# An encoder step on one core: first product between x tiles, masks after the q units, norms by pairs, the last norm's end in two passes

## The chip, the core and the metric

The kernel runs on one core of a Trainium2 chip. The metric is the device time of one execution in microseconds (us), as the median of several executions. One execution of each kernel was also taken with the hardware profiler; the views quoted are of that execution. PE is the matrix engine, PEld its weight loads, DVE, ACT and POOL the vector, scalar and general engines, SP the engine that issues most DMAs.

## The reference

One layer of a streaming encoder, on 1024 new frames of one stream and 64 frames of another, 1088 rows of 1024 columns in all. In short:

```python
z = x @ w_in                                  # 1024 -> 8200 columns
glu = z_conv[..., :E] * sigmoid(z_conv[..., E:])
dw = depthwise_conv31(concat(conv_buf, glu)) + b_dw
y_a = silu(layer_norm(dw, ln_a_g, ln_a_b)) @ w_a_out
h, C1, n1, m1 = mlstm(z_q, z_k / 16, z_v, ig, lf, C0, n0, m0)   # 4 heads of 256, chunkwise, causal decay
y_b = (sigmoid(z_o) * head_norm(h) * hn_g) @ w_b_out
merged = sigmoid(g_a) * y_a + sigmoid(g_b) * y_b
x1 = layer_norm(ALPHA * x + merged @ w_out, ln1_g, ln1_b)
ff = square(relu(x1 @ w_ff1)) @ w_ff2         # 1024 -> 4096 -> 1024
x2 = layer_norm(ALPHA * x1 + ff, ln2_g, ln2_b)
```

Everything is float32. The outputs are x2, the convolution's last 30 rows and the states C, n and m of both streams.

## The kernel before, in words

**Products.** Nearly all products are feature-major: the weights are the stationary operand, 128 output features at a time (a unit), and the moving operand is the transposed activations in three chunks of rows, 384, 384 and 320 wide (chunks 0, 1, 2). Float32 accuracy comes from splitting both operands into a high and a low part (`split`: ACT writes the high part, DVE the rest) and three matmuls for each of the eight blocks of 128 inputs (`mm3`), so a product of one unit and one chunk is 24 matmuls. `g` tiles are the three PSUM banks of products, `m` tiles five banks for transposes and small sums.

**Stages.** (1) The start: nine row tiles of x are loaded (pool `xp`, four buffers), transposed on PE and split (`start_x`); the gates' weights `wg` are a tile of the same pool. (2) The input projection, head by head: convolution units, k, q, v and o units, and between their products the chunkwise recurrence of the head (`mlstm`), the convolution on DVE and other work. `head_start` prepares a head's tiles, among them the decay mask `dt`: POOL broadcasts a row over the partitions (L386) and cuts it to a triangle, ACT takes nine exponentials. (3) The b branch's product, during which `ln_a` normalises the convolution's output; then the a branch's product. (4) The output projection (`out_proj`), whose units are the inner loop of each chunk, followed by the first norm of that chunk (`ln1`). (5) The feed-forward in blocks of four units; the first units' chunk 2 is held back until its norm is done. (6) The last block writes row-major tiles of x2 (24 matmuls of 512 columns for each of nine row tiles) with the second norm behind each (`ln_stats`, `ln2_back`).

**The feature-major norm** (`ln_feature`, for `ln_a` and `ln1`) sums over features, which lie on partitions and on eight tiles. DVE adds the eight tiles, PE sums over partitions with a matrix of 1/1024 (L690, L691 for the high and low part), DVE subtracts the mean (L699), ACT squares, DVE adds up the squares (reductions, L678), PE sums them to one column per row (L711, L714), DVE and POOL form the power −0.5 (L716, L717), DVE spreads it over a diagonal (L719), PE broadcasts it (L725, L726), and DVE and ACT scale (L729, L815). It is a generator: each `yield` hands control back for one product, and `waits` holds how many products stand ahead of each of the three PE steps.

**What sets the order.** `N` and `J` line up the jobs; a job's products call `slot()`, which moves the background generators (`mlstm`, `conv`, `misc`) on by a step. A scheduler of the framework then places the instructions on each engine's queue, in an order near that of the program; `pin` keeps an instruction at its place. Each engine works its queue strictly in that order, and waits by semaphores. SP issues the loads: x tiles, weights two units ahead (`wload`), and for `out_proj` one column block of the transposed x per product (`sx`, from pool `st`, five buffers).

Of the kernel before, what the change touches and what calls it, by code (L numbers as in the profile page):

```python
# [49 lines left out]
def hybrid_layer(ctx, tc, x_prompt, x_sample, cache_conv, state_C, state_n, state_m, w_in, b_gate,  # L50
# [101 lines left out]
    xp = pool("xp", 4, stack=st0)  # L152

# [19 lines left out]
    xt0 = [load_x(0), load_x(1)]  # L173

    def start_x():
        for i in range(3):
            trans_x(i, xt0[i])
            if i == 1:
                wsplit(0, True)
        for i in range(3, NT):  # L180
            trans_x(i, load_x(i))
# [19 lines left out]
    def gates():  # L201
# [29 lines left out]
        wg = xp.tile([P, KT, P], F32R, tag="x", name="wg")  # L231
# [78 lines left out]
    early, later = [], []  # L310
# [8 lines left out]
    def unit(hi, lo, post, chunks=(0, 1, 2)):  # L319
        for ci in chunks:  # L320
            ps = early.pop() if early and ci == 0 else product(hi, lo, ci)
# [50 lines left out]
    def head_start(h):  # L372
# [12 lines left out]
        dt = hd.tile([P, NT, P], F32, tag="dt", name="dt")  # L385
# [211 lines left out]
    for h in range(NH):  # L597
# [7 lines left out]
        for j in range(2):  # L605
            add_unit(w_in, 2048 + h * HD + j * P, post_kq("q", j, 1.0))
        for j in range(2):
            add_unit(w_in, 4096 + h * HD + j * P, post_v(j))
# [38 lines left out]
    def ln_stats(tiles, n):  # L647
# [6 lines left out]
        V.scalar_tensor_tensor(st[:n, 16:17], st[:n, 12:13], -1.0, st[:n, 15:16], ALU.mult, ALU.mult)  # L654
        return st[:n, 15:16], st[:n, 16:17]
# [14 lines left out]
    def ln_feature(y, n, sc, square, finish, waits):  # L670
# [6 lines left out]
        def total(out, t, m=CN):  # L677
            V.tensor_reduce(out[:, :n], t[:, :, :n].rearrange("p k t -> p t k"), AX.X, ALU.add)  # L678

        s2 = stp.tile([P, CN], F32, tag="st", name="s2")  # L680
        total(s2, y[:, 0:4])
        yield
        s, sh, sl = tiles()
        total(s, y[:, 4:8])
        V.tensor_tensor(s[:, :n], s[:, :n], s2[:, :n], ALU.add)
        split(sh[:, :n], sl[:, :n], s[:, :n])
# [9 lines left out]
        sq = []  # L696
        for kh in range(2):
            yh = y[:, 4 * kh:4 * kh + 4, :n]
            V.tensor_tensor(yh, yh, across(pm), ALU.subtract)  # L699
            sq.append(square())  # L700
            S.activation(sq[kh][:, :, :n], yh, AF.Square)
        total(s, sq[0])
        total(s2, sq[1])
# [105 lines left out]
    last_ln = []  # L809

    def ln1(ci):
# [12 lines left out]
        yield from ln_feature(Y2[ci], n, pools["ln1"], square, finish, ((1, 3, 2), (1, 3, 1), (1, 2, 1))[ci])  # L824
# [5 lines left out]
    def out_proj():  # L830
# [4 lines left out]
        for ci, (o, n) in enumerate(CHUNKS):  # L835
            Y2.append(fp.tile([P, KT, CN], F32, tag="f", name="y2"))
            for j in range(KT):
# [8 lines left out]
                slot()  # L846
                if ci == 2 and j == 4:
                    last_ln.append(ln1(ci))
                    next(last_ln[0])
            if ci < 2:  # L850
                BG["misc"].append(ln1(ci))
        drain("misc")
        BG["misc"].append(last_ln[0])
# [328 lines left out]
```

## Time and profile before

| | |
|---|---|
| median of three runs | 1987.09 us (1985.12 to 1988.74) |
| the profiled execution's own time | 1988.86 us |
| its span | 1986.8 us |
| PE busy | 1938.1 us, 98% |
| DVE busy | 1425.0 us, 72% |
| ACT busy | 642.8 us, 32% |
| POOL busy | 124.9 us, 6% |
| granted clock of PE, mean | 0.991 |
| last matmul ends | 16 us before the span's end |

The span is the time from the first to the last instruction. The granted clock is the share of full speed that PE was given; a matmul at half clock counts as busy for its whole length. The waits of PE are shown by the line that waited, the engine and line that it waited for, the total, the times and the longest.

### The profile page before, as it was taken

The page shows a single profiled execution, that of the slowest core. Times are in us where ns is not written, and L with a number is a line of the kernel's source. Part 1 is how long each engine was busy: PE and PEld are TensorE (multiplying, and loading weights), DVE is VectorE, ACT ScalarE, POOL GpSimd, SP SyncE. Part 2 cuts the span into 40 slices and gives each one's busy share as a digit, 9 for nine tenths or more (in the row PEclk, how much of TensorE's full clock was granted, in tenths as well). Part 3 has the DMA queues.
Part 4 walks back from the last instruction along what each step waited for, and adds up shares of the span by engine and source line. Part 5 has one row for each costly group of instructions (what it writes and reads, how often), then busy time and mean ns, then how long its engine had stood idle before and what let it go on. Part 6 is the DMA issues. An engine that isn't in the chain of part 4 may idle for free.

```text
span 1986.8 us, 30495 instructions
## 1 busy us (share of the span) xinstructions
PE 1938.1 (98%) x12396; PEld 1914.4 (96%) x12396; DVE 1425.0 (72%) x2717; ACT 642.8 (32%) x1206; POOL 124.9 (6%) x232
## 2 busy tenths in 40 slices
PE   8999999999999999999999998999999999999996
PEld 7999999999999999999999998999999999999995
DVE  3856876787678767878874559867685858677547
ACT  4323322332233223323352214523233232414242
POOL 1112210001000100000000000000000000000005
PEclk9999999999999999999999999999999999999998
DMA  4122312121112211226235210111211111111212
GB/s 140 44 79 58 119 48 57 52 74 52 55 34 66 70 55 43 60 93 205 84 102 158 76 42 14 43 54 33 59 38 54 53 44 54 33 54 43 75 43 80
DMA packets 171744, 131.06 MB, mean 66 GB/s; under 512 B 8271, under 2 KB 166463, under 8 KB 171603
## 3 DMA queue, kind: packets, MB, share of 16 engines
q1 hardware_dynamic: 171603, 129.11, 21.7%
q8 instruction: 97, 1.59, 0.3%
q14 instruction: 44, 0.36, 0.1%
HBM read 104.39 MB, written 24.63 MB: 65 GB/s over the span
## 4 chain that ended last, share of the span: by engine, by line
PE 83%; DVE 9%; issue 3%; ACT 1%; POOL 1%; DMA 1%; SPq 0%; POOLq 0%; ACTq 0%; DVEq 0%
PE g L328 26%; PE g L331 26%; PE g L332 26%; DVE s L678 2%; PE m L328 1%; PE m L332 1%; PE m L331 1%; DVE o L1101 1%; DVE acc L567 1%; DVE ln L650 0%; DVE a L699 0%; DVE y L699 0%; PE m L461 0%; DMA x<-in_x_prompt_dram 0%; PE m L1061 0%
## 5 line engine op out<-in xcount | busy, mean ns | idle before, releaser
L328 PE MATMUL g<-xh,wh 128*128 128x384 f32 (+1 forms) x1920 | 637.7, 332 | 0.0
L331 PE MATMUL g<-xl,wh 128*128 128x384 f32 (+1 forms) x1920 | 632.0, 329 | 0.0
L332 PE MATMUL g<-xh,wl 128*128 128x384 f32 (+1 forms) x1920 | 631.5, 329 | 0.0
L328 PEld LDWEIGHTS g<-xh,wh 128*128 128x128 f32 x1920 | 363.7, 189 | 0.4 <-ACT xh L336 0.2
L331 PEld LDWEIGHTS g<-xl,wh 128*128 128x128 f32 x1920 | 363.5, 189 | 0.3
L332 PEld LDWEIGHTS g<-xh,wl 128*128 128x128 f32 x1920 | 363.1, 189 | 0.1
L567 DVE SCALAR_TENSOR_TENSOR acc<-glu,vecs,acc 128x1118 f32<-128x1118 f32 x240 | 331.6, 1382 | 3.5
L336 ACT ACTIVATE wh<-wr 128x1024 fp32r<-128x1024 f32 (+1 forms) x168 | 166.0, 988 | 445.9 <-PE g L331 355.7
L339 DVE TENSOR_TENSOR wl<-wr,wh 128x1024 fp32r<-128x1024 f32 (+1 forms) x168 | 190.7, 1135 | 113.8 <-ACT wh L336 110.9
L328 PE MATMUL g<-x1h,wh 128*128 128x384 f32 (+1 forms) x768 | 253.4, 331 | 0.0
L331 PE MATMUL g<-x1l,wh 128*128 128x384 f32 (+1 forms) x768 | 253.1, 330 | 0.0
L332 PE MATMUL g<-x1h,wl 128*128 128x384 f32 (+1 forms) x768 | 252.8, 329 | 0.0
L331 PE MATMUL g<-hvl,wh 128*128 128x272 f32 x784 | 223.7, 288 | 0.0
L332 PE MATMUL g<-hvh,wl 128*128 128x272 f32 x784 | 221.9, 288 | 0.0
L328 PE MATMUL g<-hvh,wh 128*128 128x272 f32 x784 | 221.4, 290 | 0.0
L977 DVE TENSOR_TENSOR y<-g,y 128x272 f32<-128x272 f32 (+1 forms) x540 | 157.2, 340 | 26.9 <-PE g L332 25.1
L328 PEld LDWEIGHTS g<-hvh,wh 128*128 128x128 f32 x784 | 146.0, 189 | 1.7 <-DVE y L977 1.3
L331 PEld LDWEIGHTS g<-hvl,wh 128*128 128x128 f32 x784 | 147.5, 188 | 0.0
L332 PEld LDWEIGHTS g<-hvh,wl 128*128 128x128 f32 x784 | 146.5, 188 | 0.0
L331 PEld LDWEIGHTS g<-x1l,wh 128*128 128x128 f32 x768 | 144.9, 189 | 0.1
L332 PEld LDWEIGHTS g<-x1h,wl 128*128 128x128 f32 x768 | 144.9, 189 | 0.0
L328 PEld LDWEIGHTS g<-x1h,wh 128*128 128x128 f32 x768 | 144.6, 188 | 0.1
(272 smaller groups left out, 2423.6 us busy)
## 6 DMA issues: line engine op xcount, KB each, us to landing
wr<-in_w_in_dram SPq DMA_DIRECT2D x64, 512.0 KB
wr<-in_w_ff_dram SPq DMA_DIRECT2D x64, 512.0 KB
x<-in_x_prompt_dram SPq DMA_DIRECT2D x8, 512.0 KB
dwT<-acc SPq DMA_DIRECT2D x8, 512.0 KB
wr<-in_w_b_out_dram SPq DMA_DIRECT2D x8, 512.0 KB
wr<-in_w_a_out_dram SPq DMA_DIRECT2D x8, 512.0 KB
wr<-in_w_out_dram SPq DMA_DIRECT2D x8, 512.0 KB
out_dram<-o SPq DMA_DIRECT2D x16, 256.0 KB
```

The lines of the kernel that those rows point to most:

```text
L328: first = TE.matmul(out, lh, rh, start=start, stop=False, skip_group_check=more)
L331: TE.matmul(out, lh, rl, start=False, stop=False, skip_group_check=more)
L332: TE.matmul(out, ll, rh, start=False, stop=stop, skip_group_check=more)
L336: a = S.activation(hi, src, AF.Copy)
L339: V.tensor_tensor(lo, src, hi.bitcast(F32), ALU.subtract)
L567: V.scalar_tensor_tensor(acc, glu[:, j:j + AC], vecs[:, c, j:j + 1], acc, ALU.mult, ALU.add))
L678: V.tensor_reduce(out[:, :n], t[:, :, :n].rearrange("p k t -> p t k"), AX.X, ALU.add)
L977: V.tensor_tensor(y, ps[:, pslc], y, ALU.add)
L1101: V.tensor_tensor(o[:n, hs], o[:n, hs], pools["g2"][:n, hs], ALU.mult)
```

## The change

In seven places:

- **Start.** `wg` gets a pool of its own. Three x tiles are loaded before the first weights instead of two, the fourth before the second weights instead of the third. The product of the first unit and chunk 0 is issued after tile 2 of x instead of after all tiles, and is kept in `early`, which is now keyed by chunk.
- **Masks.** The decay mask leaves `head_start` and becomes `head_decay`, a job behind the head's q units.
- **Norms by pairs.** In `ln_feature` the reductions over four tiles (`total`) become pairwise additions (`fold`: one add of two tiles' width, one of one tile's), and the first sum begins with one add of four tiles to four.
- **First norm.** `out_proj` keeps a running column sum of each chunk, `ys`, with one add per product, and `ln1` starts from it. The counts in `waits` change, and the third chunk's norm starts behind the last product without a slot of its own.
- **Feed-forward.** The third unit's products of chunk 0 and of chunk 1 are both issued before the held chunk 2 products; before, only that of chunk 0.
- **Second norm.** `ln_stats` returns the mean and the power and drops the product of the two. `ln2_back` forms (y − mean) × g on DVE first, then scales on ACT, then adds b on POOL; for the eighth row tile the add is on DVE, and the ninth is done on DVE alone.

The diff:

```diff
@@ -150,6 +150,7 @@
     negM = cv.tile([P, T], F32, name="negM")
     st0 = ExitStack()
     xp = pool("xp", 4, stack=st0)
+    xg = pool("xg", 1, stack=st0)
 
     def load_x(i):
         xt = xp.tile([P, D], F32, tag="x", name="x")
@@ -170,14 +171,16 @@
             S.activation(hi, ps[:, :, :n], AF.Copy)
             V.tensor_tensor(XL[ci][:, kh * 4:kh * 4 + 4, off:off + n], ps[:, :, :n], hi.bitcast(F32), ALU.subtract)
 
-    xt0 = [load_x(0), load_x(1)]
+    xt0 = [load_x(0), load_x(1), load_x(2)]
 
     def start_x():
-        for i in range(3):
+        for i in range(4):
             trans_x(i, xt0[i])
             if i == 1:
                 wsplit(0, True)
-        for i in range(3, NT):
+            if i == 2:
+                early[0] = product(*his[0], 0)
+        for i in range(4, NT):
             trans_x(i, load_x(i))
         vp = xp.tile([NV, D], F32, tag="x", name="vp")
         nc.sync.dma_start(vp[0:CW, :], w_dw[0])
@@ -228,7 +231,7 @@
         G.memset(mask, 1.0)
         G.memset(mask[:, 0:T:P], 0.0)
         G.memset(cols[SS:, 8], 0.0)
-        wg = xp.tile([P, KT, P], F32R, tag="x", name="wg")
+        wg = xg.tile([P, KT, P], F32R, name="wg")
         G.memset(wg.bitcast(F32), 0.0)
         S.activation(wg[:, :, 0:8], wgr, AF.Copy)
         V.tensor_tensor(wg[:, :, 8:16], wgr, wg[:, :, 0:8].bitcast(F32), ALU.subtract)
@@ -307,7 +310,7 @@
             V.tensor_copy(cols[:n, b:b + nb], ps[:n, 0:nb].rearrange("p c (h z) -> p c h z", z=32)[:, :, :, 0:4])
 
 
-    early, later = [], []
+    early, later = {}, []
 
     def product(hi, lo, ci):
         n = CHUNKS[ci][1]
@@ -318,7 +321,7 @@
 
     def unit(hi, lo, post, chunks=(0, 1, 2)):
         for ci in chunks:
-            ps = early.pop() if early and ci == 0 else product(hi, lo, ci)
+            ps = early.pop(ci) if ci in early else product(hi, lo, ci)
             while later:
                 later.pop()()
             post(ci, *CHUNKS[ci], ps)
@@ -382,7 +385,9 @@
             G.memset(t[:, :, HD + 1:].bitcast(F32), 0.0)
             G.memset(t[SS:, 8, :HD].bitcast(F32), 0.0)
         HT["vh"], HT["vl"] = vh, vl
-        dt = hd.tile([P, NT, P], F32, tag="dt", name="dt")
+
+    def head_decay(h):
+        dt = pools["hd"].tile([P, NT, P], F32, tag="dt", name="dt")
         G.partition_broadcast(dt.rearrange("p c t -> p (c t)")[:, :T], negM[32 * h:32 * h + 1, :])
         G.memset(dt[:, 8, SS:], MASKED)
         G.affine_select(dt, dt, [[0, NT], [1, P]], ALU.is_ge, MASKED, base=0, channel_multiplier=-1)
@@ -604,6 +609,7 @@
             add_unit(w_in, 3072 + h * HD + j * P, post_kq("k", j, 1.0 / 16.0))
         for j in range(2):
             add_unit(w_in, 2048 + h * HD + j * P, post_kq("q", j, 1.0))
+        N(lambda h=h: head_decay(h))
         for j in range(2):
             add_unit(w_in, 4096 + h * HD + j * P, post_v(j))
         if h == 0:
@@ -651,8 +657,7 @@
         V.bn_aggr(st[:n, 12:14], st[:n, 0:12])
         G.tensor_scalar(st[:n, 14:15], st[:n, 13:14], EPS, None, ALU.add)
         G.tensor_tensor(st[:n, 15:16], st[:n, 14:15], mhalf[:n], ALU.pow)
-        V.scalar_tensor_tensor(st[:n, 16:17], st[:n, 12:13], -1.0, st[:n, 15:16], ALU.mult, ALU.mult)
-        return st[:n, 15:16], st[:n, 16:17]
+        return st[:n, 12:13], st[:n, 15:16]
 
 
     A32, MB = [], []
@@ -667,23 +672,25 @@
             MB.append(fp.tile([P, KT, CN], F32, tag="f", name="mb"))
         BG["misc"].append(ln_a())
 
-    def ln_feature(y, n, sc, square, finish, waits):
+    def ln_feature(y, n, sc, square, finish, waits, total=None):
         def across(p, k=4):
             return bcast(p[:, None, :n], [P, k, n])
 
         def tiles():
             return (sc.tile([P, CN], d, tag=t, name=t) for t, d in (("s", F32), ("sh", F32R), ("sl", F32R)))
 
-        def total(out, t, m=CN):
-            V.tensor_reduce(out[:, :n], t[:, :, :n].rearrange("p k t -> p t k"), AX.X, ALU.add)
-
-        s2 = stp.tile([P, CN], F32, tag="st", name="s2")
-        total(s2, y[:, 0:4])
-        yield
+        def fold(out, t):
+            V.tensor_tensor(t[:, 0:2, :n], t[:, 0:2, :n], t[:, 2:4, :n], ALU.add)
+            V.tensor_tensor(out[:, :n], t[:, 0, :n], t[:, 1, :n], ALU.add)
+
         s, sh, sl = tiles()
-        total(s, y[:, 4:8])
-        V.tensor_tensor(s[:, :n], s[:, :n], s2[:, :n], ALU.add)
-        split(sh[:, :n], sl[:, :n], s[:, :n])
+        if total is None:
+            t = square()
+            V.tensor_tensor(t[:, :, :n], y[:, 0:4, :n], y[:, 4:8, :n], ALU.add)
+            fold(s, t)
+            total = s
+            yield
+        split(sh[:, :n], sl[:, :n], total[:, :n])
         for _ in range(waits[0]):
             yield
         pm = mtile()
@@ -693,14 +700,12 @@
         s2 = sc.tile([P, CN], F32, tag="s2", name="s2")
         if n < CN:
             G.memset(s[:, n:], 0.0)
-        sq = []
-        for kh in range(2):
+        for kh, part in enumerate((s, s2)):
             yh = y[:, 4 * kh:4 * kh + 4, :n]
             V.tensor_tensor(yh, yh, across(pm), ALU.subtract)
-            sq.append(square())
-            S.activation(sq[kh][:, :, :n], yh, AF.Square)
-        total(s, sq[0])
-        total(s2, sq[1])
+            sq = square()
+            S.activation(sq[:, :, :n], yh, AF.Square)
+            fold(part, sq)
         V.tensor_tensor(s[:, :n], s[:, :n], s2[:, :n], ALU.add)
         split(sh, sl, s)
         for _ in range(waits[1]):
@@ -806,7 +811,7 @@
 
 
     X1H, X1L, Y2 = [], [], []
-    last_ln = []
+    YS = []
 
     def ln1(ci):
         n = CHUNKS[ci][1]
@@ -821,7 +826,7 @@
 
         def square():
             return pools["lnq" if ci == 2 else "ln1"].tile([P, 4, CN], F32, tag="sq", name="sq")
-        yield from ln_feature(Y2[ci], n, pools["ln1"], square, finish, ((1, 3, 2), (1, 3, 1), (1, 2, 1))[ci])
+        yield from ln_feature(Y2[ci], n, pools["ln1"], square, finish, ((2, 3, 2), (2, 3, 2), (1, 2, 1))[ci], YS[ci])
         if ci == 2:
             lnq.close()
             lns.close()
@@ -843,14 +848,15 @@
                     mm3(ps[:, :n], WOH[j // 4][:, k, js], WOL[j // 4][:, k, js], MH[ci][:, k, :n], ML[ci][:, k, :n],
                         k == 0, k == KT - 1)
                 V.scalar_tensor_tensor(Y2[ci][:, j, :n], s[:, :n], ALPHA, ps[:, :n], ALU.mult, ALU.add)
-                slot()
-                if ci == 2 and j == 4:
-                    last_ln.append(ln1(ci))
-                    next(last_ln[0])
-            if ci < 2:
-                BG["misc"].append(ln1(ci))
-        drain("misc")
-        BG["misc"].append(last_ln[0])
+                if j == 1:
+                    YS.append(stp.tile([P, CN], F32, tag="st", name="ys"))
+                if j:
+                    V.tensor_tensor(YS[ci][:, :n], Y2[ci][:, 0, :n] if j == 1 else YS[ci][:, :n], Y2[ci][:, j, :n], ALU.add)
+                if ci < 2 or j < KT - 1:
+                    slot()
+            if ci == 2:
+                drain("misc")
+            BG["misc"].append(ln1(ci))
         step("misc")
 
     N(out_proj)
@@ -1000,7 +1006,8 @@
             pools["whl"] = pools["whl2"]
             third = 2 + next(i for i, p in enumerate(pieces) if p[3] == 1)
             wsplit(third)
-            early.append(product(*his[third], 0))
+            for ci in range(2):
+                early[ci] = product(*his[third], ci)
             drain("misc")
             for h in held:
                 unit(*h, (2,))
@@ -1092,15 +1099,24 @@
             prev = (i, y, *stats)
         ln2_back(*prev)
 
-    def ln2_back(i, y, rstd, nmr):
+    def ln2_back(i, y, mean, rstd):
         n = tile_len(i)
         o = pools["ln2"].tile([P, D], F32, tag="o", name="o")
         for hf in range(2):
             hs = slice(hf * 512, hf * 512 + 512)
-            S.activation(o[:n, hs], y[:, hs], AF.Identity, bias=nmr, scale=rstd)
-            V.tensor_tensor(o[:n, hs], o[:n, hs], pools["g2"][:n, hs], ALU.mult)
-            (V if i == NT - 1 and hf == 1 else G).tensor_tensor(o[:n, hs], o[:n, hs], pools["b2"][:n, hs], ALU.add)
-            nc.sync.dma_start(y_prompt[0, i * P:(i + 1) * P, hs] if i < 8 else y_sample[0, :, hs], o[:n, hs])
+            if i < NT - 1:
+                V.scalar_tensor_tensor(o[:n, hs], y[:, hs], mean, pools["g2"][:n, hs], ALU.subtract, ALU.mult)
+                S.activation(o[:n, hs], o[:n, hs], AF.Identity, scale=rstd)
+                (V if i == NT - 2 else G).tensor_tensor(o[:n, hs], o[:n, hs], pools["b2"][:n, hs], ALU.add)
+            else:
+                V.scalar_tensor_tensor(o[:n, hs], y[:, hs], mean, pools["g2"][:n, hs], ALU.subtract, ALU.mult)
+                if hf == 1:
+                    for h2 in range(2):
+                        hs = slice(h2 * 512, h2 * 512 + 512)
+                        V.scalar_tensor_tensor(o[:n, hs], o[:n, hs], rstd, pools["b2"][:n, hs], ALU.mult, ALU.add)
+                        nc.sync.dma_start(y_sample[0, :, hs], o[:n, hs])
+                continue
+            nc.sync.dma_start(y_prompt[0, i * P:(i + 1) * P, hs], o[:n, hs])
 
     N(open_last)
     for u in range((NBLK - 1) * NB, NBLK * NB):
@@ -1137,7 +1153,7 @@
 
     idx = 0
     wload(0)
-    xt0.append(load_x(2))
+    xt0.append(load_x(3))
     wload(1)
     for ap, fn, kind, _ in jobs:
         if ap is None:
```

The order of POOL around the second head's start, first before, then of the change. `dt` is the head's mask, `st` the row statistics of the previous head's last tile, `xs` a sum that is written back to memory, `nout` and `vh` state and value tiles.

```order
L377 MEMSET k 128x2x64
L386 ISA
L386 ISA dt<-negM 128x1088
L508 COPY nout<-C 128x2
L364 ISA
L364 TENSOR_TENSOR xs<-xh,xl 128x320
L520 TENSOR_SCALAR st<-st 64x1
L364 TENSOR_TENSOR xs<-xh,xl 128x320
L521 TENSOR_TENSOR st<-st,mhalf 64x1
L381 MEMSET vh 128x9
```

```order
L380 MEMSET k 128x2x64
L391 ISA
L391 ISA dt<-negM 128x1088
L513 COPY nout<-C 128x2
L367 ISA
L367 TENSOR_TENSOR xs<-xh,xl 128x320
L525 TENSOR_SCALAR st<-st 64x1
L367 TENSOR_TENSOR xs<-xh,xl 128x320
L526 TENSOR_TENSOR st<-st,mhalf 64x1
L384 MEMSET vh 128x9
```

The same rows stand at the same places; the line of the mask's broadcast is L391 now, that of the statistics L525 and L526.

The order of DVE in the norm of branch a, chunk 1, from the subtraction of the mean on, before and then of the change. `a` is the chunk (the last tile number is the next chunk), `sq` the squares, `s`, `sh`, `sl` the sum and its parts, `mb` the merged product beside it.

```order
L699 TENSOR_TENSOR a_9287<-a_9287,m 128x1536 x2
L678 TENSOR_REDUCE s<-sq 128x384
L678 TENSOR_REDUCE s_9764<-sq 128x384
L763 TENSOR_TENSOR mb<-g,sb 128x384
L704 TENSOR_TENSOR s<-s,s_9764 128x384
L763 TENSOR_TENSOR mb<-g,sb 128x320
L678 TENSOR_REDUCE s_9953<-a_9289 128x320
L339 TENSOR_TENSOR sl<-s,sh 128x384
L339 TENSOR_TENSOR wl<-wr,wh 128x1024
L763 TENSOR_TENSOR mb<-g,sb 128x384
```

```order
L705 TENSOR_TENSOR a_9291<-a_9291,m 128x1536 x2
L683 TENSOR_TENSOR sq<-sq 128x768
L768 TENSOR_TENSOR mb<-g,sb 128x384
L684 TENSOR_TENSOR s<-sq 128x384
L683 TENSOR_TENSOR sq<-sq 128x768
L689 TENSOR_TENSOR sq<-a_9293 128x4x320
L684 TENSOR_TENSOR s_9770<-sq 128x384
L768 TENSOR_TENSOR mb<-g,sb 128x320
L709 TENSOR_TENSOR s<-s,s_9770 128x384
L342 TENSOR_TENSOR wl<-wr,wh 128x1024
L342 TENSOR_TENSOR sl<-s,sh 128x384
L683 TENSOR_TENSOR sq<-sq 128x2x320
```

Two reductions of the squares and one over the next chunk became pairwise adds; the next chunk's first add (L689) moved ahead of the sum of the squares, and the weight split `wl` ahead of `sl`.

The order of ACT where the output projection ends and the feed-forward begins. `y_11265` and `y_11283` are chunk 1 of the first norm, the higher number chunk 2, `x1h` the high part of the normed chunk, `wh` that of a weight, `r` the relu of a product.

```order
L336 ACTIVATE x1h<-y_11265 128x768
L815 ACTIVATE y_11265<-y_11265,vecs 128x384 x2
L336 ACTIVATE x1h<-y_11265 128x768
L815 ACTIVATE y_11265<-y_11265,vecs 128x384 x2
L336 ACTIVATE x1h<-y_11265 128x768
L815 ACTIVATE y_11265<-y_11265,vecs 128x384
L336 ACTIVATE sh<-s 128x320
L336 ACTIVATE x1h<-y_11265 128x768
L336 ACTIVATE wh<-wr 128x1024
L906 ACTIVATE r<-g 128x384
L336 ACTIVATE wh<-wr 128x1024
L701 ACTIVATE sq<-y_11558 128x4x320 x2
```

```order
L820 ACTIVATE y_11283<-y_11283,vecs 128x384 x2
L339 ACTIVATE sh<-ys 128x320
L339 ACTIVATE x1h<-y_11283 128x768
L820 ACTIVATE y_11283<-y_11283,vecs 128x384 x3
L339 ACTIVATE x1h<-y_11283 128x768
L820 ACTIVATE y_11283<-y_11283,vecs 128x384 x2
L339 ACTIVATE x1h<-y_11283 128x768
L820 ACTIVATE y_11283<-y_11283,vecs 128x384
L339 ACTIVATE wh<-wr 128x1024
L339 ACTIVATE x1h<-y_11283 128x768
L339 ACTIVATE wh<-wr 128x1024
L912 ACTIVATE r<-g 128x384
```

The scaling of chunk 1 is split in the same way in both. The high part of chunk 2's sum (`sh<-s 128x320`, now `sh<-ys 128x320`) moved from behind the chunk's last scaling to behind its second. On PE the broadcast that this scaling waits for moved too: it stood 16 matmuls into chunk 2's last product and the rest of that product followed it, and now it stands behind the whole product.

## The prediction

> **What bounds the kernel now.** I read the page's busy times first, then what PE waited for, then the chain at each wait, then the last 40 us.
>
> ```profile
> span 1986.8 us, 30495 instructions
> PE 1938.1 (98%) x12396; PEld 1914.4 (96%) x12396; DVE 1425.0 (72%) x2717; ACT 642.8 (32%) x1206; POOL 124.9 (6%) x232
> ```
>
> PE sets the end. The change leaves its 12396 matmuls as they are, so it can gain only what PE does not spend on matmuls at full clock: 1986.8 − 1938.1 = 48.7 us idle, and the stretches at half clock, which count as busy. The waits of PE by line (us in total, how often, the longest):
>
> ```profile
> PE m L445 <- DVE isb L523: 7.0, 3, 2.5
> PE m L168 <- DMA x<-in_x_prompt_dram: 6.6, 3, 4.8
> PE m L714 <- DVE sl L339: 4.8, 3, 2.3
> PE m L711 <- ACT sh L336: 4.7, 2, 2.9
> PE m L725 <- ACT sh L336: 2.0, 2, 1.6
> PE g L240 <- DVE wg L234: 1.2, 1, 1.2
> ```
>
> L445 is the start of a head, L168 the transposes of x, L240 the gates, and L711, L714 and L725 are steps of the two feature-major norms. Most of the longer waits cost a second time. One wait and the window behind it, and two windows behind other waits (length, PE's busy time, its matmuls, the granted clock):
>
> ```profile
> core 0: us, PE busy (x), PEclk, DMA share, GB/s
> 258.50:260.97 2.47, 0.00 (x1) 1.00 0.33 119
> 260.97:264.38 3.41, 3.41 (x20) 1.00 0.68 164
> 468.24:471.65 3.41, 3.41 (x12) 0.50 0.00 0
> 1178.21:1181.62 3.41, 3.41 (x12) 0.50 0.17 48
> ```
>
> Behind the waits at 465 and at 1175 the clock is 0.50 for one window of 3.41 us: 12 matmuls where 20 fit at full clock, so a window loses 3.41/2 = 1.7 us. There are seven such windows before the last matmul, each behind an idle time of 1.6 us or more; they lie on a grid of 3.41 us, and the wait of 2.5 at 258.5 has none, so one that straddles two windows can escape. [...]
>
> **Start (gain 2, from 0 to 4).** The gate weights get a buffer of their own, so the 1.2 us at L240 go, and with them the half window at 31.35 (1.7). Against that, the first product now stands behind 34 transposes. The last two of these belong to x4, which moves from the seventh transfer of the queue to the ninth, behind both weight loads and the gates' weights.
>
> ```profile
> 10.00:17.50 7.50, 6.35 (x29) 5.81 (x28) 4.94 (x7) 4.42 (x8) 0.00 (x0) 1.00 0.88 332
> ```
>
> At 332 GB/s a 512 KB tile takes 1.6 us, so PE stands still about 1.6 longer before x4. Its transposes and first matmuls run at half speed there (the warm-up ends at 17.68), so that time is worth 0.8 of work at full clock. 1.2 + 1.7 − 0.8 = 2.1. Both ends are a window of 1.7 more or less, since the warm-up can fall on another window.
>
> **Head masks (0).** The chain into a head's first products:
>
> ```profile
> 454.35 1.37 POOL dt L386
> 456.50 6.83 issue
> 463.33 1.11 POOL st L520
> 465.79 1.33 DVE isb L523
> 467.17 0.33 PE m L445 x2
> ```
>
> The last tile's row statistics (st) of the previous head sit behind the broadcast that begins the next head's mask (dt), 9 us earlier on POOL. The code moves the mask behind the q units, but in the order of POOL (shown above) the broadcast still precedes that st, with the same rows between them. The three waits (7.0) and two half windows (3.4) stay.
>
> **Norm of branch a (gain 6.4, from 4 to 6.8).** In this stage PE waited 4.8 − 2.3 = 2.5 at L714, 2.0 at L725 and 0.5 at L726, and lost one half window. The view of DVE there and two groups of its forms, and one row of its timeline:
>
> ```profile
> L678 DVE TENSOR_REDUCE s<-sq x12: 2427/2911/2962, 941.3 to 1237.3; 128x384 f32<-128x1536 f32 x8, 128x320 f32<-128x1280 f32 x4
> L729 DVE TENSOR_TENSOR a<-a,m 128x768 f32<-128x768 f32 x8 | 7.1, 947 | 0.0
> L704 DVE TENSOR_TENSOR s<-s,s 128x384 f32<-128x384 f32 x2 | 1.1, 548 | 0.0
> 980.38 2.36 DVE L678 TENSOR_REDUCE s<-a 128x320 f32<-128x1280 f32 x1
> ```
>
> A reduction over four tiles takes 2.91; two pairwise adds take 0.95 + 0.55 = 1.50. The first sum becomes one 1536-wide add (at most 2 × 0.95 = 1.9) and a fold, 3.4 for 2 × 2.91 + 0.55 = 6.4. The squares' two reductions give up 2 × 1.41 = 2.8. Per chunk DVE is 5.8 us shorter. Where PE waited longest, 2.1 at L714, the split sl stood behind the next chunk's reduction (2.36, from 980.38). In the new order a 1280-wide add (1.6) takes that reduction's place, the squares' folds are 2.8 shorter, and a weight split (1.2) now stands ahead: 0.8 + 2.8 − 1.2 = 2.4 earlier, a little more than was waited. 5.0 + 1.7 = 6.7, less 0.3 where slack is thin. Low end: the half window remains at another place and 1 us of waits.
>
> **Norm 1, first two chunks (gain 9.1, from 5 to 9.1).** The waits in two stretches of the output projection, 1170 to 1182 and 1195 to 1222:
>
> ```profile
> PE m L714 <- DVE sl L339: 2.3, 1, 2.3
> PE m L711 <- ACT sh L336: 2.9, 1, 2.9
> PE m L690 <- ACT sh L336: 0.8, 1, 0.8
> ```
>
> The column sums now grow tile by tile beside the products: 24 adds at most 0.55 long, each under a product of 24 matmuls (24 × 3.41/20 = 4.1 us), so they cost nothing. A norm then starts with its split, and the squares' fold is 2.8 shorter. The counts of products that stand ahead of L690 and of L725 grow as well, which is more cover. Waits 2.3 + 0.8 + 2.9 and the two half windows go: 6.0 + 3.4, less 0.3.
>
> **Start of the feed-forward (loss 3.5, from −6 to +1).** The longer counts push chunk 1's broadcast (L725/L726) from inside the last product of the projection to behind it. There before:
>
> ```profile
> 1226.00:1248.00 22.00, 18.08 (x95) 17.22 (x94) 19.02 (x20) 10.54 (x17) 1.85 (x2) 0.92 0.15 48
> PE m L690 <- ACT sh L336: 1.9, 1, 1.9
> PE m L711 <- ACT sh L336: 1.8, 1, 1.8
> L339 DVE TENSOR_TENSOR x1l<-y,x1h 128x768 fp32r<-128x768 f32 x8 | 7.6, 956 | 0.3
> L815 ACT ACTIVATE y<-y,vecs 128x384 f32<-128x384 f32 x16 | 10.4, 696 | 12.0 <-DVE y L729 12.0
> L336 ACT ACTIVATE x1h<-y 128x768 fp32r<-128x768 f32 x8 | 6.7, 832 | 0.0
> ```
>
> 3.7 us of the waits stand here, 0.3 at L691 come to it, and one half window: 5.7. After, counting from T, where PE passes L725: DVE scales four pairs (0.95 each, T+3.9), and only then splits (x1l). PE does 24 matmuls and is at T+4.4; the mean over chunk 2 then waits for sl, queued behind the first x1l, until T+5.4: 1.0. The next product takes chunk 1's own x1h and x1l by pairs, and each pair of columns needs two L815 (0.65 each) and one x1h (0.83) on ACT, then 0.95 on DVE; PE uses a pair in 1.04: waits of 0.6, 1.0 and 1.5. Behind the last x1l DVE has, for chunk 2's squares, two subtractions (320/384 of 1.9, so 1.6 each), two folds (1.25 each), a weight split of 1024 columns (1.2), two relu products (0.5 each) and the sum (0.5): 8.4 us, while PE has one pair and one whole product left (5.2), so L711 waits 3.2. Together 1.0 + 3.1 + 3.2 = 7.3, with one half window 9.0 against 5.7, and 0.2 for handing on between the engines: 3.5. Low end: two more half windows fall here. High end: L711's wait is covered by the products that stand ahead of it.
>
> **One more product ahead (0).** The held third-chunk products (320 wide) are now run in a row behind two units' first products. They are the same 72 matmuls, and they need x1 of chunk 2, which by then has had two more products to finish. If it is late, the price lies in the range just given.
>
> **Last norm (gain 7, from −2 to 8).** The end of DVE, ACT and POOL:
>
> ```profile
> 1966.78 0.16 DVE L654 SCALAR_TENSOR_TENSOR ln<-ln 128x1 f32<-128x1 f32 x1 [1.07 <-POOL ln L653]
> 1967.82 0.69 DVE L1101 TENSOR_TENSOR o<-o,g 128x512 f32<-128x512 f32 x1 [0.28 <-ACT o L1100]
> 1969.03 1.40 DVE L1101 TENSOR_TENSOR o<-o,g 128x512 f32<-128x512 f32 x1
> 1973.07 0.16 DVE L654 SCALAR_TENSOR_TENSOR ln<-ln 128x1 f32<-128x1 f32 x1 [1.07 <-POOL ln L653]
> 1974.88 3.45 POOL L1102 TENSOR_TENSOR o<-o,b 128x512 f32<-128x512 f32 x2 [1.85 <-DVE o L1101]
> 1981.65 1.63 DVE L1102 TENSOR_TENSOR o<-o,b 64x512 f32<-64x512 f32 x1
> 1940.00:1971.00 31.00, 30.97 (x134) 24.80 (x132) 24.09 (x40) 7.62 (x10) 16.55 (x21) 1.00 0.21 81
> 1971.00:1987.00 16.00, 0.00 (x0) 0.00 (x0) 8.20 (x15) 3.04 (x4) 7.52 (x8) 0.58 0.23 76
> ```
>
> DVE needs 1973.07 − 1966.78 = 6.29 a tile, for it waits on POOL (1.07) and on ACT (0.28), and one product by g lasts 1.40, not 0.69, while POOL adds b. PE needs 24 matmuls of 30.97/134 = 0.231 a tile, 5.55, runs ahead and ends at 1971.0 (E), so the tail is 15.8. After, the product needs only the mean, which DVE has itself: two adds, two halves of statistics and two products, about 0.69 each, and 0.2 to join them: 4.3 a tile; with 0.6 of collision on each product 5.5, which is still not over PE. DVE then ends with the tile: the last add, statistics, two products, POOL's power and two more products come to about E+4.6, and 3.5 from the last operation to the end (1983.28 to 1986.8) makes E+8.1; with some lag E+8.8. 15.8 − 8.8 = 7.
>
> **Sum.** 2 + 0 + 6.4 + 9.1 − 3.5 + 0 + 7 = 21.0 us. The profiled execution took 1988.86, 1.77 over the median of the runs (1987.09), and 2.06 of it lie around the span. 1988.86 − 21.0 = 1967.9, or 1966.1 from the median. I forecast **1966.5**.
>
> **Rivals.**
> - *The half windows do not follow the waits* but fall on the grid for a reason of their own. Then the start's, branch a's and norm 1's two windows stay: 4 × 1.7 = 6.8, so 1973. Against it: all seven windows stand behind a wait of 1.6 to 2.9 us. For it: one wait of 2.5 at 258.5 left the clock at full, so phases count. Chance 0.12. [...]
> - *POOL's adds stop DVE in the last norm.* The 1.40 row shows they can. If both products of a tile wait out a whole add (1.29), the cycle is 4.3 + 2.6 = 6.9, 1.3 over PE; over eight tiles the lag is 10.4, the end E+18, and the 7 gained become 2 lost: 1975.5. Against it: one of each two products ran at 0.69. Chance 0.15.
> - *The masks do leave POOL's way.* Then 7.0 + 3.4 go too: 1956. For it only the text of the code, against it the order. Chance 0.05.
> - *Slower: x starves in the output projection.* The running sum holds one of five "st" buffers through a chunk, and the column of x for each product is loaded into the same pool. With four left, a load issues three products (12.4 us) ahead. Should one take over 12.4, each of 24 products would wait for it; from 0.9 us each (24 × 0.9 = 21.6) the whole gain is gone, and 2 us each would give 1966.5 + 48 = 2014. Against it: the DMA engines are at 0.17 in the projection's window from 1178.21, and 512 KB took 1.6 at the start. Chance 0.03.
>
> **How the numbers follow.** Forecast 0.65. Its own range, with terms partly at their ends, is 1961 to 1973. To hold 8 in 10 I reach to 1958 below and to 1976, which takes in the first two rivals. About 0.2% (4 us) is what a measurement can tell from no change. All cases but the last are 10 us or more faster: faster 0.94, within 0.2% 0.03, for several low ends at once, slower 0.03.
>
> **What would show it.** Right: no wait at L240's product; the three head waits of 2.3 still there; none over 0.5 in branch a and the projection's first two chunks; a cluster of waits on x1l and sh, 4 to 8 us in all, in the first 25 us of the feed-forward; three or four half windows in all; 8 to 9 us between the last matmul and the end. Wrong: waits of DVE for POOL over 0.6 in the last 40 us, or waits for x in the projection.

## The result, and the profile after

The changed kernel takes 1965.8 us (median of four runs, 1962.42 to 1967.58) against 1987.9 before: ratio 0.9887, 95% interval 0.9871 to 0.9904, so 22.1 us less. The forecast was 1966.5. The profiled execution took 1964.53, its span 1962.7. All times are of fast executions; left out are one of the kernel before (9983.52) and one with the new start (6722.57), which took several times as long.

The page's first lines, then the waits of PE (us in total, times, the longest):

```profile
span 1962.7 us, 30510 instructions
PE 1930.5 (98%) x12396; PEld 1908.2 (97%) x12396; DVE 1389.7 (71%) x2735; ACT 637.7 (32%) x1203; POOL 123.0 (6%) x229
```

```profile
PE m L169 <- DMA x<-in_x_prompt_dram: 8.5, 3, 4.4
PE m L450 <- DVE isb L528: 6.7, 3, 2.3
PE m L716 <- ACT sh L339: 2.9, 1, 2.9
PE g L334 <- DVE x1l L342: 1.5, 2, 1.0
PE m L698 <- DVE sl L342: 1.0, 1, 1.0
```

The lines L690, L711 and L725 of before are L697, L716 and L730 here, L445 is L450. All waits of branch a's norm and of the first norm's first two chunks are gone, with that of the gates. The head waits stand, and at the start of the feed-forward there is the new cluster: 1.0 at L698, 1.5 at the first products on x1l, 2.9 at L716.

The spans of both executions, cut at the starts of certain matmuls (us, read from the two timelines):

| stretch | before | after | difference | forecast |
|---|---|---|---|---|
| start to the first v tile's transposes | 116.3 | 113.1 | −3.2 | −2 |
| to branch a's first mean (the heads) | 821.1 | 820.7 | −0.4 | 0 |
| to the output projection's first product | 178.0 | 170.2 | −7.8 | −6.4 |
| to the first product on x1 | 108.5 | 98.7 | −9.8 | −9.1 |
| to the feed-forward's first second-layer product | 55.3 | 59.4 | +4.1 | +3.5 |
| to the end of the last matmul | 691.8 | 692.4 | +0.7 | 0 |
| to the end | 15.9 | 8.2 | −7.6 | −7 |

Each stretch moved the way and about as far as forecast; only the last but one, forecast unchanged, grew by 0.7. How the runs bear that out, and where they do not, is told below.

### The profile page after: what moved, and what is told of

It is laid out like the page before. It is cut to its first block, busy times and chain, and to the rows that moved or that the text cites. A ratio compares the mean times of both kernels' runs of the same rounds, so it can differ in the third digit from the quotient of the medians.

```text
span 1962.7 us, 30510 instructions
## 1 busy us (share of the span) xinstructions
PE 1930.5 (98%) x12396; PEld 1908.2 (97%) x12396; DVE 1389.7 (71%) x2735; ACT 637.7 (32%) x1203; POOL 123.0 (6%) x229
## 4 chain that ended last, share of the span: by engine, by line
PE 91%; DVE 5%; issue 2%; POOL 1%; ACT 1%; DMA 0%; SPq 0%; DVEq 0%; POOLq 0%; ACTq 0%
PE g L331 28%; PE g L334 28%; PE g L335 28%; PE m L331 1%; PE m L335 1%; PE m L334 1%; DVE acc L572 1%; PE m L466 0%; PE m L1068 0%; PE m L413 0%; PE m L472 0%; DVE wl L342 0%; PE m L450 0%; DVE isb L528 0%; DVE C L504 0%
```

## The experiments

Unless said otherwise a time is a median, each beside runs of the kernel before on the same chip. The experiments ran on three chips; the kernel before took 1987.3, 1987.8 and 1987.9 there, so times from different chips are set against each other as they are.

**The last norm alone.** The kernel before with the new `ln_stats` return and `ln2_back`:

```diff
-        return st[:n, 15:16], st[:n, 16:17]
+        return st[:n, 12:13], st[:n, 15:16]
...
-            S.activation(o[:n, hs], y[:, hs], AF.Identity, bias=nmr, scale=rstd)
-            V.tensor_tensor(o[:n, hs], o[:n, hs], pools["g2"][:n, hs], ALU.mult)
+                V.scalar_tensor_tensor(o[:n, hs], y[:, hs], mean, pools["g2"][:n, hs], ALU.subtract, ALU.mult)
+                S.activation(o[:n, hs], o[:n, hs], AF.Identity, scale=rstd)
```

> The kernel before with the last norm's new end alone (mean and power kept apart, product by g first, b added by DVE in the eighth tile, ninth on DVE). Theory 1 (the parts of the change add up, and this one is worth what the last 40 us lost between the two traces): the time from the last matmul to the end falls from 15.8 to about 8.2, nothing else moves: 7.6 us less than the kernel before, 1980.3. Theory 2 (the end was shortened by the other parts too, which left POOL or the DMA queue free earlier): 3 to 5 less.

1980.4 (1978.98 to 1981.68), 7.5 less; ratio 0.997, interval 0.9959 to 0.9982. From the last matmul to the end it is 7.95. The timelines of DVE and POOL in the changed kernel show a whole tile:

```profile
1941.61 0.69 DVE L656 BATCH_NORM_STATS2 ln<-yt 128x6 f32<-128x512 f32 x1
1943.34 0.69 DVE L1095 TENSOR_TENSOR yt<-g,yt 128x512 f32<-128x512 f32 x1 [1.04 <-PE g L335]
1944.07 0.69 DVE L656 BATCH_NORM_STATS2 ln<-yt 128x6 f32<-128x512 f32 x1
1944.80 0.21 DVE L657 BATCH_NORM_AGGREGATE ln<-ln 128x2 f32<-128x12 f32 x1
1945.10 1.42 DVE L1108 SCALAR_TENSOR_TENSOR o<-yt,ln,g 128x512 f32<-128x512 f32 x2
```

```profile
1941.51 2.55 POOL L1110 TENSOR_TENSOR o<-o,b 128x512 f32<-128x512 f32 x2 [0.84 <-ACT o L1109]
1945.09 0.22 POOL L658 TENSOR_SCALAR ln<-ln 128x1 f32<-128x1 f32 x1 [1.04 <-DVE ln L657]
1945.40 0.88 POOL L659 TENSOR_TENSOR ln<-ln,mhalf 128x1 f32<-128x1 f32 x1
```

DVE waits for nothing but PE (1.04), so PE is the bound. POOL's two adds (1941.51 to 1944.06) fall on DVE's statistics, its wait and the add from PSUM, not on its products, which last 0.75 each on the average. The rival in which POOL stops DVE is out.

**Pairwise adds in branch a alone.** The kernel before; `ln_a` uses the new sums, the first norm keeps its reductions:

```diff
-            yield from ln_feature(A32[ci], n, ln, square, finish, (1, 3, 1))
+            yield from ln_pairs(A32[ci], n, ln, square, finish, (1, 3, 1))
```

> The kernel before with pairwise adds in the norm of branch a alone; the first norm keeps its reductions. Theory 1 (the 5.1 us of waits and the half window there come from DVE's reductions): this stage loses 6.5 to 7.8 us, as between the two traces, all else stays: 1980 to 1981.5. Theory 2 (part of the stage's gain came from the weight splits and merged products being ordered otherwise by the other edits): 3 to 5 less. A half window more or less elsewhere, 1.7, is possible under both.

1979.5 (1977.61 to 1981.27), 8.4 less; ratio 0.9963, interval 0.9952 to 0.9975. The stretch falls from 178.0 to 170.2, as in the full change, so the pairwise adds alone are the cause there.

**The start alone, and the start taken back.** First the kernel before with the new start (own pool for `wg`, loads, first product behind tile 2). Then the kernel of 1946.5 us (the second under "Both", below) with the old start:

```diff
-    xt0 = [load_x(0), load_x(1), load_x(2)]
+    xt0 = [load_x(0), load_x(1)]
...
-            if i == 2:
-                early[0] = product(*his[0], 0)
```

> The kernel before with the new start alone (own buffer for the gates' weights, other order of the loads, first product between the x tiles). Theory 1 (worked out in the prediction, 2.1 less, and seen between the two traces as 2.8 up to the first v tile): 2 to 3.2 less, 1985 to 1986. Theory 2 (the start only looked shorter because of where the warm-up's window fell in that execution): within 1 us of the kernel before.

> The fastest kernel so far (changed kernel, broadcast of chunk 1 two products earlier, mask behind the statistics, 1946.5) with the start of the kernel before put back. Alone on the kernel before, the new start gave no difference (ratio 1.0002, interval 0.9992 to 1.0012), though its traces are 2.8 to 3.2 us shorter up to the first v tile. Here no later wait is long enough for a half window, so nothing behind the start can answer to where it leaves the clock's windows. Theory 1 (the new start is worth its 3 us and the runs alone hid it in the later half windows): 2 to 3.5 us slower, 1948.5 to 1950. Theory 2 (the start is worth nothing in most executions, the profiled ones were lucky): within 1 us of 1946.5.

Alone: 1987.9, ratio 1.0002, interval 0.9992 to 1.0012, so no gain shows, and the 2 us forecast (a ratio of 0.999) lie just outside the interval. Taken back: 1947.1 (1946.52 to 1949.93) against 1946.5 (1945.97 to 1947.28), 0.6 more. Yet in both profiled executions the start differs, by 3.2 and 3.8 us up to the first v tile, and so it does in all thirteen traces of this case: 115.7 to 116.7 us with the old start (four traces), 112.7 to 114.3 with the new one (nine). The old start's clock in the second experiment (length, PE's busy time, its matmuls, that of PEld, DVE, ACT, POOL, the granted clock, the DMA engines' share and GB/s):

```profile
18.00:31.70 13.70, 12.54 (x89) 11.50 (x89) 7.13 (x15) 7.03 (x13) 5.58 (x6) 1.00 0.36 84
31.76:35.17 3.41, 3.41 (x12) 3.40 (x12) 0.06 (x1) 0.75 (x1) 0.00 (x0) 0.50 0.42 124
```

The wait for the gates' weights and its half window are there as before. But that profiled execution was the longest of its four (1949.93), and the one of the new start alone the shortest of its ten (1983.38; its heads are 2.6 shorter than before too). Without these two executions the medians are 1946.8, 0.3 more than with the new start, and 1987.9. So the difference shows in the executions whose traces were kept, and hardly in the others. What the start does in those others can't be seen here, and stays open.

**Chunk 1's broadcast one product earlier.** The changed kernel with one number put back:

```diff
-        ... ((2, 3, 2), (2, 3, 2), (1, 2, 1))[ci], YS[ci])
+        ... ((2, 3, 2), (2, 3, 1), (1, 2, 1))[ci], YS[ci])
```

> The changed kernel with one number put back: the first norm's chunk 1 broadcasts its power one product earlier, ahead of the projection's last product and not behind it. Theory 1 (the cluster of waits at the start of the feed-forward, 5.4 us and two half windows, comes from this place, since the scaling and splitting of chunk 1 begins behind the broadcast): chunk 1 is scaled 3.6 us earlier, so the waits for x1l (1.5) and for the mean of chunk 2 (1.0) go and the 2.9 at the third step shrinks to about 1 or less; with it at least one of two half windows. Expected 3.5 to 7 us less than the changed kernel, 1959 to 1962.5, unless the broadcast itself now waits, which would show as a wait at L730. Theory 2 (the cluster comes from the amount of work on DVE and ACT there, wherever it begins): the waits only change place, within 1.5 us of the changed kernel.

1958.9 (1958.12 to 1960.05), 6.9 less than the changed kernel. The stretch falls from 59.4 to 52.5, the mean granted clock rises from 0.993 to 0.996 in all four runs, and two waits are left:

```profile
PE m L716 <- ACT sh L339: 1.8, 1, 1.8
PE m L697 <- ACT sh L339: 1.0, 1, 1.0
```

So 2.6 of the cluster's 5.4 us of waits came from where the broadcast stood, not from the amount of work. The other 4.3 of the 6.9 leaves room for both half windows (2 × 1.7 = 3.4, an estimate from the changed kernel's windows), and the higher clock speaks for it. 2.8 of the waits stayed, more than expected: chunk 2's mean still waits 1.0, now for the high part of its sum, and the third step 1.8 instead of about 1 or less.

**The mask really behind the statistics.** The changed kernel; both POOL instructions of the broadcast follow the last head's statistics on its queue:

```diff
+        for i in nc.cur_bb.bb.instructions:
+            if last_st and i.name not in seen and i.engine == cast.ins.engine:
+                tc.add_manual_dep(i, last_st[0].ins.name, ...)
```

> The changed kernel with the mask's broadcast made to follow, on POOL's queue, the last row statistics of the previous head. Theory 1 (the three head waits come from the broadcast in front of those statistics): the waits at L450's transposes, 6.7 us in all, fall to under 0.5 each, and the two half windows behind them (3.4) go: about 10 us less than the changed kernel, 1956. Theory 2 (the statistics would be late anyway, by the memsets and other additions that share POOL): most of the 6.7 stays, within 3 us of the changed kernel. A third outcome is that the later mask makes the next head's first products wait, as a wait of PE for the exponentials.

1954.9 (1954.23 to 1955.53), 10.9 less than the changed kernel. The chain of the second head in the changed kernel, and POOL's timeline there in this one:

```profile
453.05 6.60 issue
459.65 1.18 POOL st L525
460.99 0.31 POOL vl L386
461.38 0.60 POOL st L526
```

```profile
451.79 0.21 POOL L533 TENSOR_SCALAR st<-st 64x1 f32<-64x1 f32 x1 [0.74 <-DVE st L532]
452.08 0.56 POOL L534 TENSOR_TENSOR st<-st,mhalf 64x1 f32<-64x1 f32 x1
458.64 1.36 POOL L394 PARTITION_BROADCAST dt<-negM  x1 [6.00 <-issue]
```

The statistics run at 451.8, not 459.7, and the broadcast's 6 us of issue come behind them, where PE waits for none of it. The waits at the heads are gone from the list of PE's waits, and the heads' stretch falls from 820.7 to 810.7.

**Both, and chunk 1 a product earlier still.** The two edits together, and then also the mean of chunk 1 one product sooner:

```diff
-        ... ((2, 3, 2), (2, 3, 1), (1, 2, 1))[ci], YS[ci])
+        ... ((2, 3, 2), (1, 3, 1), (1, 2, 1))[ci], YS[ci])
```

> The changed kernel with both single edits: chunk 1's broadcast one product earlier (6.9 us less alone) and the mask's broadcast behind the previous head's statistics (10.9 less alone). Theory 1 (the stages are independent, PE is the bound everywhere): the two add up, 1965.8 - 17.8 = 1948, with 1.7 either way for where half windows fall. Theory 2 (what one stage gives the other partly takes back): 1950 or more.

> As the kernel with both edits, and chunk 1 of the first norm starts its mean one product earlier too, so its broadcast stands three products ahead of the projection's end, where the change as made had it one and a half behind. Theory 1 (what is left at the start of the feed-forward, waits of 1.0 and 1.75, comes from chunk 1's scaling and splitting still running when chunk 2's norm begins): both waits fall below 0.5, with any half window there: 2 to 4 us less than the kernel with both edits. Theory 2 (those waits are chunk 2's own chain from the last product through sum, split, mean, squares): no difference over 1 us. A wait at the mean of chunk 1 (L705) would show that its sum is not ready one product earlier.

1950.1 (1948.22 to 1952.6) and 1946.5 (1945.97 to 1947.28). The first is 15.7 less than the changed kernel, 2 short of the sum of 17.8 and where theory 2 begins. In its profiled execution, the shortest (1948.22), both stretches are what they were in the single edits (810.8 and 52.6), so there they add. Of the two longer executions no trace was kept, but the mean granted clock of each is on record: 0.995 (1952.6) and 0.996 (1951.35), against 0.998 in the two shorter. That is about 6 and 4 us of clock; they are 4.1 and 2.9 us longer, so lost clock is enough to account for it, though where it was lost isn't shown. The second is 3.5 less than the first. At its start of the feed-forward one wait of 0.8 is left, where under 0.5 was expected, and one of 0.8 came at the broadcast of chunk 1:

```profile
PE m L724 <- ACT sh L339: 0.8, 1, 0.8
PE m L738 <- ACT sh L339: 0.8, 1, 0.8
```

The long middle of that execution in one window (length, PE, PEld, DVE, ACT and POOL busy, the granted clock):

```profile
40.00:1940.00 1900.00, 1891.00 (x12204) 1871.72 (x12202) 1374.42 (x2705) 622.08 (x1178) 118.01 (x214) 1.00 0.22 65
```

Between 40 and 1940 PE is busy for 1891 of 1900 us and the mean granted clock is 1.00.

**One more product ahead taken back**, on this last kernel:

```diff
-            for ci in range(2):
-                early[ci] = product(*his[third], ci)
+            early[0] = product(*his[third], 0)
```

> The fastest kernel so far with the one more product ahead taken back: the third unit's product of chunk 1 stands behind the held third chunks again. Theory 1 (the prediction: it is worth nothing where the third chunk's norm is done in time): within 1 us of 1946.5. Theory 2 (it covers the third chunk's scaling and splitting): a wait of PE for x1l or x1h of chunk 2 appears at the held products, up to 4 us, one product's length.

1945.2 (1945.01 to 1946.53), 1.3 less, with ranges that overlap. No wait appears at the held products, so the extra product hides nothing. The traces show that it costs a little. Where it stands, the changed kernel included, PE waits for DVE at the start of the second layer; in this kernel and in the kernel before that wait is missing:

```profile
PE g L331 <- DVE y L981: 0.5, 2, 0.3
```

From the first second-layer product to the last matmul it is 691.6 us here against 692.7 with the extra product. Over all traces it is 691.6 to 691.9 without it (five) and 692.4 to 693.1 with it (eight), and that is the 0.7 which the table above shows. This is the fastest kernel: ratio 0.9788 to the kernel before, interval 0.9774 to 0.9801.

**Useless matmuls in a wait.** Twice the changed kernel with matmuls added whose result nobody reads: 12 at each head's start, and 15 ahead of the step of chunk 2 that waited 2.9 us:

```diff
+                pin(TE.matmul(pd[:, :CN], mean1, XH[0][:, 0, :CN], start=True, stop=True))
...
+                pin(TE.matmul(pd[:, :CN], mean1, fill[:, 0, :CN], start=True, stop=True))
```

> The changed kernel with 12 extra matmuls of 384 columns on PE (2.1 us, their result is read by nobody) in the place of each of the three head waits. The statistics are as late as before. Theory 1 (the half windows follow from PE's idle time in the window): PE has work in the 2.3 us in which it waited, so the waits and the two half windows behind them go and the extra matmuls take the waits' place: the stretch from the first v tile to branch a's norm is 3 to 4 us shorter than in the changed kernel, about 1962. Theory 2 (half windows fall there for another reason): the clock is at half in the same places, and the time stays within 1 us of the changed kernel.

> The changed kernel with 15 extra matmuls of 384 columns (2.6 us, read by nobody) right ahead of the step of the first norm's chunk 2 at which PE waited 2.9 us, behind which two windows ran at half clock. The norm itself is as late as before. Theory 1 (the half clock follows from PE being idle for most of a window): the wait shrinks to about 0.3 to 0.9, the two half windows go, and the stretch from the feed-forward's first product to its second stage falls from 59.4 to 56 to 56.6, although PE does more work: about 1962.5 in all. Theory 2 (the half windows have another cause): 59.4 stays within 0.5, or grows.

The first failed as a test: 1971.2. The scheduler moved the head's transposes ahead of as many of the next product's matmuls as were added, so the three waits of 2.3 stayed, and the added work cost its own time on PE (36 matmuls, 0.17 each, 6.2 us). The second did what it should. The windows at that place, the changed kernel first (columns as for the old start's clock):

```profile
1219.20:1222.66 3.46, 0.70 (x4) 0.38 (x3) 3.35 (x6) 0.94 (x2) 0.00 (x0) 1.00 0.07 13
1222.66:1226.07 3.41, 3.28 (x12) 3.28 (x13) 0.72 (x2) 0.07 (x1) 0.21 (x1) 0.50 0.41 141
1226.07:1229.48 3.41, 3.41 (x12) 3.41 (x12) 1.12 (x2) 0.52 (x1) 0.63 (x1) 0.50 0.00 0
```

```profile
1219.20:1222.60 3.40, 3.40 (x22) 3.40 (x21) 3.37 (x7) 1.13 (x2) 0.00 (x0) 1.00 0.00 0
1222.60:1226.00 3.40, 2.74 (x17) 2.34 (x16) 1.51 (x4) 0.52 (x1) 0.75 (x1) 1.00 0.51 154
1226.00:1229.40 3.40, 3.40 (x22) 3.40 (x21) 1.12 (x2) 0.71 (x2) 0.10 (x1) 1.00 0.00 0
```

With 15 matmuls more, both windows run at 1.00 where 0.50 stood and the stretch is 56.8 instead of 59.4, though the norm is as late as it was. In all it is 1963.3 (1962.25 to 1965.23). Ahead of them PE is idle for 2.76 of 3.46 us in the changed kernel and for 0.00 of 3.40 here: the half clock went with PE's idle time, and the rival that it falls where it will is out.

## Why the prediction was right, point by point

- **What bounds it, and the sum.** PE, with its waits and the half windows behind them. Measured alone the end is worth 7.5 and branch a 8.4; the first norm and the feed-forward's start come to 9.8 − 4.1 = 5.7 by the traces and the heads to 0.4: 22.0 together, less the 0.7 that the extra product ahead costs: 21.3, against 22.1 measured and 21.0 forecast.
- **Start: this step failed.** In the traces the forecast mechanism is there: x waits rose from 6.6 to 8.5, the wait at L240 and its half window went, 3.2 in all. What the forecast calls the warm-up shows there as PE's pace: in the changed kernel's trace matmuls of 384 columns start 0.32 apart up to 17.7 us and 0.17 to 0.18 from there, and in that of the kernel before one lasts 0.61 at 17.28 and 0.42 at 18.08; neither shows the pace change at another place. But in the runs the start is worth 0.0 and 0.6, not 2. It fits that the two profiled executions lie 24.3 apart and the medians only 22.1. Why the executions without a kept trace don't show it stays open. Without this term the forecast would have been a gain of 19.0, and 22.1 came: the other terms were 3 too small together, so that the sum came out as near as 1.1 is partly luck.
- **Head masks: right.** The order decided, not the place in the code (in the changed kernel's trace POOL ran the rows in the order shown for it: L391 at 244.58, L513 at 246.01, L367 at 253.26, L525 at 254.13): 7.0 of waits became 6.7, with two half windows (464.90 and 673.11). The rival in which the masks leave POOL's way had the right price: 10.9 measured where 10.4 stood, once the broadcast was really moved.
- **Branch a: right cause, 6.4 was too small**, and so was the upper end of 6.8: 7.8 in the trace. The term that was probably missing: in the trace a matmul lasts 0.33 but the next starts 0.17 behind it, so a wait counted from end to start leaves out 0.16 of lost overlap. Five waits make 0.8: 5.1 + 1.7 + 0.8 = 7.6. This is worked out, with matmul ends that the trace only models; no run tests it apart.
- **Norm 1: right**, 9.8 for 9.1; three such overlaps would make 0.5 of the difference.
- **Start of the feed-forward: right, 4.1 lost for 3.5.** Waits of 1.0, 0.6, 1.0, 1.5 and 3.2 were worked out, 7.3 in all; 1.0, none, 0.6, 0.9 and 2.9 came, 5.4. The splits on DVE, with T, where PE passes the broadcast of chunk 1, at 1202.3:

```profile
1207.67 0.48 DVE L342 TENSOR_TENSOR sl<-ys,sh 128x320 fp32r<-128x320 f32 x1
1208.88 0.96 DVE L342 TENSOR_TENSOR x1l<-y,x1h 128x768 fp32r<-128x768 f32 x1 [0.73 <-ACT x1h L339]
1210.82 0.96 DVE L342 TENSOR_TENSOR x1l<-y,x1h 128x768 fp32r<-128x768 f32 x1 [0.98 <-ACT x1h L339]
1213.51 0.95 DVE L342 TENSOR_TENSOR x1l<-y,x1h 128x768 fp32r<-128x768 f32 x1
```

  `sl` is done at T+5.9, 0.5 later than worked out, while the x1l stand where they were expected (the second ends at T+7.5), so each of their waits is about 0.5 shorter. In their place two windows ran at half clock where one had been counted.
- **One more product ahead: right that nothing is gained**, but it was put at 0 and costs about 1: 0.7 to 1.2 in that stretch of the traces, 1.3 in the runs.
- **Last norm: right**, 7.6 and 7.5 for 7.
- **Slower by starved loads of x: out.** PE and DVE wait for no such load; the projection is 9.8 shorter.

## What to carry to other kernels

Price a wait of PE with the half window behind it (1.7 us here) and with the lost overlap (0.16 here, an estimate), and look where the edit puts the next wait: here a count of products that was raised to cover one wait made a cluster of four behind it. Where a scheduler orders the queues, moving a call in the code may move nothing; read the order on the engine that is late, and tie the instruction to the one it has to follow. A term that shows in a trace should be timed alone, over several executions, before it is counted.

## What the runs showed of the hardware that was not expected

In the traces of the kernel before and of the changed kernel the half clock went with PE's idle time inside one window of 3.41 us, not with the length of a wait. The changed kernel's first and second head wait about the same, 2.18 and 2.27. Windows on the grid on which the half windows lie (PE's busy time, the granted clock):

```profile
253.27:256.69 3.42, 1.94 (x12) 1.00 0.13 48
256.69:260.10 3.41, 2.71 (x16) 1.00 0.77 200
260.10:263.51 3.41, 3.41 (x22) 1.00 0.14 50
461.49:464.90 3.41, 1.33 (x8) 1.00 0.59 154
464.90:468.31 3.41, 3.41 (x13) 0.50 0.00 0
```

The first straddles two windows, 1.48 and 0.70 idle, and no window at 0.50 follows; the second lies in one, 2.08 idle, and the next window is at 0.50. Between 40 us and the last matmul, the windows on that grid with the most idle time are these. Before: 2.30, 2.26, 2.24, 2.14, 2.00 and 1.62, each followed by one window at 0.50, then 1.55 and 1.53, followed by none. In the changed kernel: 2.75, followed by two, 2.08 and 1.75, each followed by one, then 1.48, followed by none. The start doesn't fit in: before, the half window at 31.35 stands behind a window with 1.22 idle, so that six of the seven, not all, stand behind 1.6 or more, as the forecast has it. Why a second window follows the 2.75, and why one follows 1.62 and none 1.55, isn't shown.

Around the mask's broadcast on POOL, 1.36 us at 450.91 in the changed kernel, the traces have longer stretches of issue. In the changed kernel the trace has two records of POOL's sequencer for each mask's broadcast, and two for the statistics at each of the second and the third head wait:

```profile
L391 POOLq MODIFY_POOL_CONFIG  x8: 6/10/11, 44.0 to 652.9; - x8
L525 POOLq MODIFY_POOL_CONFIG  x4: 4/4/4, 453.0 to 660.8; - x4
```

At the second wait 6.60 us of issue lie between the second of these records (453.05) and the statistics (459.65), while a copy and three memsets ran from 452.34 to 452.99, right behind the broadcast (450.91 to 452.27). With the mask behind the statistics 6.00 us of issue stand ahead of the broadcast, and the cut to a triangle follows it at 460.08, within 0.1 us. What POOL does in these 6.60 and 6.00 us the traces don't show.
